# Low parts of the attention's weights by an adding transfer from DRAM

## The chip, the cores and the metric

One core of a Trainium2 chip runs the whole program. The metric is the device time of one execution in microseconds (us). Five engines work side by side, each through its own list of instructions in order: TensorE (PE, and PEld for its weight loads), VectorE (DVE), ScalarE (ACT), GpSimd (POOL) and SyncE (SP). SP, ACT and POOL also issue DMA transfers.

## What is computed

Two network blocks over 256 tokens of width 1024: a block with a latent attention (MLA) and a state-space layer (S5), then a block with a mixer, a cross attention and a feed-forward part. The change lies in the MLA layer, whose projections are

```python
q_dn, kv_dn, k_rope, gate = jnp.split(h @ w_in, MLA_SPLITS, axis=-1)
q = (_rmsnorm(q_dn, q_norm) @ w_uq).reshape(b, n, MLA_HEADS, MLA_NOPE + MLA_ROPE)
q_abs = jnp.einsum('bnhd,chd->bnhc', q[..., :MLA_NOPE], w_uk)
...
return (v * jax.nn.silu(gate)) @ w_out
```

## The kernel before

Matrix products of float32 are made of three passes on PE: every operand is split into a high part (`hi`, rounded to the float32r type) and a low part (`lo = x - hi`), and `mm` (L116 to L121) adds hi*hi, lo*hi and hi*lo, one matmul a line (L119, L120, L121).

A weight tile is 128x1024 (512 KB). `weight` (L88) takes it in: SP loads `wr` from DRAM (three buffers), ACT writes `wh` (L97), DVE subtracts `wl = wr - wh` (L98). `wh` and `wl` have two buffers each in the ring "w", so the tiles of a weight are free for the next but one only when its last matmul is done.

The MLA layer has two stages. In `mla_in` 16 gate tiles are made, each by 24 matmuls of 512 columns over one weight (`linear`, tile `lin`), then ACT takes the result (`sg`, L738) and SP stores it. In `mla_heads` 16 heads are worked on, with one weight of `hp` for two heads (`pair_in`, tile `qrope` first) and the first twelve weights of `w_out1` (`mla_out`). That makes 16 + 8 + 12 = 36 weights.

Beside it runs the preparation of the S5 layer, `s5_prep`, cut into pieces that `side` puts between the gates and heads. One pass (16 in all) loads `sp_x`, and for each of two directions d makes two outer products on DVE: `sp_r`, and `sp_o`, a single buffer of which ACT writes one slice (L390) and DVE the rest, and which SP stores to DRAM as `d_o`. Then PE transposes `sp_r` (tile `rtps`, L400), ACT copies that out (`sp_rt`, L404, two buffers, stored as `d_rt`), and PE multiplies `sp_o` with `sp_r` (tile `gps`, L413). After the second direction ACT copies `gps` to `sp_g` (L419), and POOL issues eight stores `d_t` of 64 KB (L427).

PE keeps the order of the program (`self.ordered`): gate, the modulation's matmuls `modps`, `rtps`, `gps`, the next gate, and so on, one direction a gate. The order on DVE, ACT, POOL and SP is the framework's list scheduler's, by priority; the outer products stand at a lower priority (`behind`).

Of the kernel before, what the change touches and what calls it, by code (L numbers as in the profile page):

```python
# [11 lines left out]
F32 = mybir.dt.float32  # L12
# [7 lines left out]
ADD, SUB, MUL, MAX, MIN = ALU.add, ALU.subtract, ALU.mult, ALU.max, ALU.min  # L20
# [8 lines left out]
class InOrder:  # L29


    def __init__(self, net, engine):
        self.net, self.engine = net, engine
# [6 lines left out]
class Net:  # L40
    def __init__(self, tc, ctx, I, out):
        self.tc, self.nc, self.ctx, self.I, self.out = tc, tc.nc, ctx, I, out
        self.dram = ctx.enter_context(tc.tile_pool(name="scratch", bufs=1, space=DRAM))
        self.gp = ctx.enter_context(tc.tile_pool(name="glob", bufs=1))
        self.big = ctx.enter_context(tc.tile_pool(name="big", bufs=1))
        self.ordered = ()
        nc = self.nc
        self.ident = self.gp.tile([128, 128], F32, name="ident")
        make_identity(nc, self.ident)
        self.ones = {}  # L50
        for n in (1, 1024, 512):
            t = self.gp.tile([128, 128], F32, name=f"ones{n}")
            nc.gpsimd.memset(t, 1.0 / n)
            self.ones[n] = t
# [33 lines left out]
    def weight(self, src, keep=None):  # L88


        nc = self.nc
        pool, tag, bufs = keep or self.rings[0]
        self.rings.append(self.rings.pop(0))
        raw = self.wp.tile([128, 1024], F32, tag="wr", name="wr", bufs=self.nwts[0])
        hi, lo = (pool.tile([128, 1024], F32R, tag=tag + x, name=tag + x, bufs=bufs) for x in "hl")
        nc.sync.dma_start(raw, src)
        self.in_order(nc.scalar.copy(hi, raw))  # L97
        self.in_order(nc.vector.tensor_tensor(lo, raw, hi.bitcast(F32), SUB))  # L98
        return hi, lo

    def split(self, hi, lo, x):
# [976 lines left out]
    def s5_layer(self, h1):  # L1078
# [3 lines left out]
        with self.tc.tile_pool(name="s5", bufs=1) as tp:  # L1082
# [52 lines left out]
            for b, (nu, early, late) in enumerate(((5, 0, 1), (3, 0, 1), (2, 1, 1), (0, 12 - NG, 0))):  # L1135
# [8 lines left out]
                for a in range(max(nu, 4 if prev else 0)):  # L1144
                    if a < nu:
                        u(*next(todo))
                        run(scan, 4.0)
                    for _ in range((early + 3 - a) // 4):
                        gate(1)
                        run(scan, 2.6)  # L1150
                    if prev and a < 4:
                        within(a)
                        across(a)
                        run(scan, 2.7)
# [422 lines left out]
    def run(self):  # L1577
        nc, tc, I = self.nc, self.tc, self.I
        self.s5_scratch()
        self.d_sg = self.dram.tile([16, 128, 512], F32, name="d_sg")  # L1580
        z = self.big.tile([128, 8, 512], F32, tag="s16", name="z", bufs=3)
        m0, m1 = (self.gp.tile([128, 24, 2], F32, name=f"mod{i}") for i in range(2))
        merged = ExitStack()
        merged.enter_context(self.phase((3, 2), ps=6, bg=2))
        with tc.tile_pool(name="prep", bufs=1) as prep:
            self.cond()

            def background():
                for k in range(16):
                    yield from self.s5_prep(k, prep)  # L1590

            def mods():
                yield from self.mod(0, [1], m0, prep)
                yield from self.mod(1, [0, 1], m1, prep)

            pieces, rest, due = background(), mods(), [D0, 0]

            def side(n):

                next(rest, None)  # L1600
                due[0] += n
                while due[0] >= 0.5 and due[1] < 64 - 2 * NL:
                    due[0] -= 0.5
                    due[1] += 1
                    if next(pieces):
                        break

            def step():
                with self.pinned("DVE"):
                    next(pieces, None)  # L1610

            with tc.tile_pool(name="lamp", bufs=1) as lp:
                lam = self.s5_lambda(self.s5_lambda_in(lp), prep, lp)

                def beside(n):
                    for _ in range((2, 1, 1, 2)[n]):
                        next(lam)

                self.ordered = (mybir.EngineType.PE, mybir.EngineType.DVE, mybir.EngineType.Activation)
                with tc.tile_pool(name="mod0", bufs=1) as mp:  # L1620
                    act, first = self.start(z, m0, mp, beside)
                self.ordered = (mybir.EngineType.PE,)
                with self.behind():
                    for _ in lam:
                        pass
                    self.s5_consts(prep)
            self.cos = self.load(self.gp, I["cos"], [128, 256], "cos")
            self.sin = self.load(self.gp, I["sin"], [128, 256], "sin")
            self.qnw = self.load(self.gp, I["q_norm"], [128, 2], "qnw")
            nc.vector.tensor_scalar(self.qnw, self.qnw, MLA_SCALE, None, MUL)  # L1630
            self.kvn = self.load(self.gp, I["kv_norm"], [128, 1], "kvn")
            side(1)
            with tc.tile_pool(name="mla", bufs=1) as mla:
                q = self.mla_in(z, act, first, mla, side)
                with tc.tile_pool(name="mlah", bufs=1) as tp:
                    vg = self.mla_heads(z, m0, q, tp, side)
            d_x1 = self.dram.tile([128, 8, 256], F32, name="d_x1")
            for _ in rest:
                pass
            with tc.tile_pool(name="ln", bufs=1) as tp:  # L1640
                h1 = self.ln_mod(z, vg, m0, m1, d_x1, tp, step)
            for _ in pieces:
                pass
        with tc.tile_pool(name="ops", bufs=1) as self.ops:
            y = self.s5_layer(h1)
        res = merged.enter_context(tc.tile_pool(name="res", bufs=1))
        x1 = res.tile([128, 8, 256], F32, name="x1")
        nc.sync.dma_start(x1, d_x1)
        with tc.tile_pool(name="mem", bufs=1) as mp:
            K, V, fill, norm = self.mem_kv(mp)  # L1650
            self.ordered = (mybir.EngineType.PE,)
            self.rings.append((mp, "w", 2))
            with tc.tile_pool(name="glu", bufs=1) as tp:
                self.glu(y, m1, x1, tp, fill, norm)
            g = self.load(mp, I["xa_g"], [128, 8], "xag")
            with tc.tile_pool(name="att", bufs=1) as ap:
                fg = self.load(mp, I["ffn_g"], [128, 8], "ffg")
                first = self.pre(x1, g, ap, X_SCALE)
                with tc.tile_pool(name="mix", bufs=1) as tp:
                    self.mixer(x1, tp, fill, first[1])  # L1660
                with tc.tile_pool(name="up", bufs=1) as fp:
                    second = self.pre(x1, fg, fp)
                    with tc.tile_pool(name="xat", bufs=1) as tp:
                        self.xattn(x1, K, V, tp, first[0], first[1], first[2], fill, second[1])
                    with tc.tile_pool(name="ffn", bufs=1) as tp:
                        g = tp.tile([128, 1024], F32, name="fing")
                        nc.sync.dma_start(g, I["fin_g"].partition_broadcast(128))
                        acc, h = self.ffn(x1, tp, second[0], second[1], second[2])
                        self.final(h, acc, g, tp)
        merged.close()  # L1670
# [119 lines left out]
```

## Time and profile before

| | us |
|---|---|
| median of 3 runs | 1449.93 (1447.34 to 1457.54) |
| the profiled execution | 1449.68 |
| its span, first to last instruction | 1447.9 |

| engine | busy, us | share of the span |
|---|---|---|
| PE | 1328.2 | 92% |
| DVE | 1150.6 | 79% |
| ACT | 712.2 | 49% |
| POOL | 102.9 | 7% |

The profile lists, for each group of instructions, its line in the code, engine and tiles (out<-in), the count, the busy time and the mean duration, and the engine's idle time before them with what ended it. Views of the trace give the same for a stretch of time; a stretch is named by its microseconds from the start of the span. The gates of `mla_in` run from 57 to 203 us, the heads from 207 to 511 us.

### The profile page before, as it was taken

The page shows a single profiled execution, that of the slowest core. Times are in us where ns is not written, and L with a number is a line of the kernel's source. Part 1 is how long each engine was busy: PE and PEld are TensorE (multiplying, and loading weights), DVE is VectorE, ACT ScalarE, POOL GpSimd, SP SyncE. Part 2 cuts the span into 40 slices and gives each one's busy share as a digit, 9 for nine tenths or more (in the row PEclk, how much of TensorE's full clock was granted, in tenths as well). Part 3 has the DMA queues.
Part 4 walks back from the last instruction along what each step waited for, and adds up shares of the span by engine and source line. Part 5 has one row for each costly group of instructions (what it writes and reads, how often), then busy time and mean ns, then how long its engine had stood idle before and what let it go on. Part 6 is the DMA issues. An engine that isn't in the chain of part 4 may idle for free.

```text
span 1447.9 us, 31095 instructions
## 1 busy us (share of the span) xinstructions
PE 1328.2 (92%) x12512; PEld 1196.9 (83%) x12512; DVE 1150.6 (79%) x2123; ACT 712.2 (49%) x1308; POOL 102.9 (7%) x225
## 2 busy tenths in 40 slices
PE   5879979999999988988768699999999999999997
PEld 4656657888888887888757599999998999999996
DVE  7999888998888899389898766555578876888887
ACT  4424436765656536322333264444347556655554
POOL 0012221111001100111111000000000000000000
PEclk9989988999999998999898899999999999999999
DMA  9469996665455544797778665655555453555552
GB/s 347 165 197 282 294 280 168 183 178 157 156 159 158 163 124 154 236 315 256 256 269 298 252 228 181 209 196 193 189 166 180 154 182 103 179 188 188 189 183 96
DMA packets 140625, 291.40 MB, mean 201 GB/s; under 512 B 30480, under 2 KB 70080, under 8 KB 135104
## 3 DMA queue, kind: packets, MB, share of 16 engines
q1 hardware_dynamic: 108592, 232.01, 48.2%
q0 software_dynamic: 11360, 49.34, 10.9%
q10 hardware_dynamic: 20528, 8.06, 2.1%
q8 instruction: 98, 1.61, 0.4%
q14 instruction: 47, 0.39, 0.1%
HBM read 234.83 MB, written 54.53 MB: 200 GB/s over the span
## 4 chain that ended last, share of the span: by engine, by line
PE 67%; DVE 20%; DMA 7%; issue 3%; ACT 3%; SPq 0%; DVEq 0%; ACTq 0%
PE lin L120 14%; PE lin L121 14%; PE lin L119 14%; DVE s_t L493 4%; DVE wl L98 3%; PE vps L472 2%; DVE s_V L495 2%; DMA sp_x<-in_s_bcw_dram 2%; DVE sp_t L37 2%; DMA mraw<-in_w_mod_dram 1%; PE dn L121 1%; PE dn L119 1%; PE dn L120 1%; DMA d_o<-sp_o 1%; DVE s_V L497 1%
## 5 line engine op out<-in xcount | busy, mean ns | idle before, releaser
L97 ACT CAST wh<-wr 128x1024 fp32r<-128x1024 f32 x268 | 280.7, 1049 | 405.4 <-PE lin L120 258.0
L98 DVE TENSOR_TENSOR wl<-wr,wh 128x1024 fp32r<-128x1024 f32 x268 | 327.6, 1223 | 146.3 <-ACT wh L97 145.6
L119 PE MATMUL lin<-prH,wh 128*128 128x256 f32 x512 | 145.3, 284 | 0.0
L119 PE MATMUL lin<-yaH,wh 128*128 128x256 f32 x512 | 144.9, 283 | 0.0
L120 PE MATMUL lin<-yaL,wh 128*128 128x256 f32 x512 | 144.7, 283 | 0.0
L121 PE MATMUL lin<-prH,wl 128*128 128x256 f32 x512 | 143.7, 281 | 1.0 <-DVE wl L98 1.0
L120 PE MATMUL lin<-prL,wh 128*128 128x256 f32 x512 | 144.1, 281 | 0.4 <-DVE prL L109 0.2
L121 PE MATMUL lin<-yaH,wl 128*128 128x256 f32 x512 | 144.2, 282 | 0.0
L120 PEld LDWEIGHTS lin<-prL,wh 128*128 128x128 f32 x512 | 96.6, 189 | 2.1 <-DVE prL L109 1.0
L119 PEld LDWEIGHTS lin<-yaH,wh 128*128 128x128 f32 x512 | 97.6, 191 | 0.0
L121 PEld LDWEIGHTS lin<-yaH,wl 128*128 128x128 f32 x512 | 97.5, 190 | 0.0
L119 PEld LDWEIGHTS lin<-prH,wh 128*128 128x128 f32 x512 | 96.7, 189 | 1.0
L120 PEld LDWEIGHTS lin<-yaL,wh 128*128 128x128 f32 x512 | 97.4, 190 | 0.0
L121 PEld LDWEIGHTS lin<-prH,wl 128*128 128x128 f32 x512 | 96.2, 188 | 1.2 <-DVE wl L98 1.2
L493 DVE TENSOR_TENSOR s_t<-s_V,s_tab 128x256 f32<-128x256 f32 (+2 forms) x120 | 73.1, 652 | 16.0 <-ACT s_V L475 14.7
L121 PE MATMUL u<-h,wl 128*128 128x256 f32 x224 | 64.1, 286 | 9.7 <-DVE wl L98 9.6
L121 PE MATMUL lin<-h,wl 128*128 128x256 f32 x128 | 43.2, 338 | 32.2 <-DVE wl L98 32.2
L427 POOL DMA_DIRECT2D d_t<-sp_g x128 | 67.0, 531 | 59.6 <-DVE sp_g L37 55.4
L119 PE MATMUL u<-h,wh 128*128 128x256 f32 x224 | 64.0, 286 | 0.0
L120 PE MATMUL u<-h,wh 128*128 128x256 f32 x224 | 63.3, 283 | 0.0
L119 PE MATMUL lin<-hH,wh 128*128 128x512 f32 x144 | 60.9, 423 | 0.7 <-ACT hH L103 0.7
L37 DVE TENSOR_TENSOR sp_t<-s_pb,sp_x 128x1024 f32<-128x1024 f32 x64 | 59.9, 953 | 0.6
(505 smaller groups left out, 3837.2 us busy)
## 6 DMA issues: line engine op xcount, KB each, us to landing
wr<-in_glu_dram SPq DMA_DIRECT2D x64, 512.0 KB, 3.3
wr<-in_w_up_dram SPq DMA_DIRECT2D x44, 512.0 KB, 3.3
wr<-in_w_in_dram SPq DMA_DIRECT2D x32, 512.0 KB, 4.8
mraw<-in_w_mod_dram SPq DMA_DIRECT2D x64, 256.0 KB, 3.3
d_rt<-sp_rt SPq DMA_DIRECT2D x64, 256.0 KB, 4.1
d_o<-sp_o SPq DMA_DIRECT2D x32, 512.0 KB, 4.7
wr<-in_s_in_dram SPq DMA_DIRECT2D x32, 512.0 KB, 4.4
s_op<-d_o POOLq DMA_DIRECT2D x16, 1024.0 KB, 7.3
```

The source lines that it names most:

```text
L37: return lambda *a, **k: self.net.in_order(f(*a, **k))
L97: self.in_order(nc.scalar.copy(hi, raw))
L98: self.in_order(nc.vector.tensor_tensor(lo, raw, hi.bitcast(F32), SUB))
L119: self.in_order(t.matmul(out, a[0], b[0], start=start, stop=False))
L120: self.in_order(t.matmul(out, a[0], b[1], start=False, stop=False))
L121: self.in_order(t.matmul(out, a[1], b[0], start=False, stop=stop))
L427: nc.gpsimd.dma_start(self.d_t[k].rearrange("s i j e c -> i s j e c")[:, :, j, e], a)
L472: self.in_order(nc.tensor.matmul(p[64 * e:64 * e + 64, c:c + 64], rt[:, d, j, r, 64 * e:64 * e + 64], u, start=True, stop=True, skip_group ...
L493: go(v.tensor_tensor(t[:, x], src.to_broadcast([128, 2, 32, n]), a[x].unsqueeze(1).to_broadcast([128, 2, 32, n]), MUL))
L495: go(v.tensor_tensor(dst, dst, t[:, 0], ADD))
L497: go(v.tensor_tensor(dst[:, 1], dst[:, 1], t[:, 1, 0], ADD))
```

## The change

While the MLA layer is issued (a flag that `run` sets around `mla_in` and `mla_heads`), DVE no longer makes `wl`. ACT writes `wl = -wh`, and POOL issues a transfer from the weight's place in DRAM that adds the weight onto `wl`. All other weights are made as before.

```diff
-        self.ordered = ()
+        self.ordered, self.adding = (), False
...
         self.in_order(nc.scalar.copy(hi, raw))
-        self.in_order(nc.vector.tensor_tensor(lo, raw, hi.bitcast(F32), SUB))
+        if self.adding:
+
+            nc.scalar.mul(lo, hi.bitcast(F32), -1.0)
+            nc.gpsimd.dma_start(lo, src, accum_op=ADD)
+        else:
+            self.in_order(nc.vector.tensor_tensor(lo, raw, hi.bitcast(F32), SUB))
         return hi, lo
...
+            self.adding = True
             with tc.tile_pool(name="mla", bufs=1) as mla:
                 q = self.mla_in(z, act, first, mla, side)
                 with tc.tile_pool(name="mlah", bufs=1) as tp:
                     vg = self.mla_heads(z, m0, q, tp, side)
+            self.adding = False
```

Lines of before from L99 on stand five further down (L390 is L395, L427 is L432). PE's order stays. The scheduler's order on the other engines moves.

On ACT, in the gates, one pass of `s5_prep` (two directions, so two gates) read before:

```order
L390 ACTIVATE sp_o<-sp_x 128x8x16
L97 CAST wh<-wr 128x1024
L738 ACTIVATE sg<-lin 128x512
L404 COPY sp_rt<-rtps 128x512 x2
L390 ACTIVATE sp_o<-sp_x 128x8x16
L97 CAST wh<-wr 128x1024
L738 ACTIVATE sg<-lin 128x512
L404 COPY sp_rt<-rtps 128x512 x2
L357 ACTIVATE sp_x<-sp_x 128x2x64
L419 COPY sp_g<-gps 128x240 x2
```

and reads now:

```order
L395 ACTIVATE sp_o<-sp_x 128x8x16
L97 CAST wh<-wr 128x1024
L743 ACTIVATE sg<-lin 128x512
L409 COPY sp_rt<-rtps 128x512 x2
L100 ACTIVATE wl<-wh 128x1024
L97 CAST wh<-wr 128x1024
L743 ACTIVATE sg<-lin 128x512
L409 COPY sp_rt<-rtps 128x512 x2
L100 ACTIVATE wl<-wh 128x1024
L395 ACTIVATE sp_o<-sp_x 128x8x16
L424 COPY sp_g<-gps 128x240 x2
L362 ACTIVATE sp_x<-sp_x 128x2x64
```

The negation (L100) stands behind the two copies of `rtps`, and the slice of `sp_o` for the second direction, which stood ahead of `wh`, now stands behind the second negation. `gps` of that direction reads the slice. The pattern is there for seven passes or parts of one.

On POOL, between two passes, stood before (`sp_r` is a small fill of the single buffer of that name):

```order
L385 MEMSET sp_r 128x16 x2
L427 DMA d_t<-sp_g 16x8x128 x8
L385 MEMSET sp_r 128x16 x2
L427 DMA d_t<-sp_g 16x8x128 x8
L385 MEMSET sp_r 128x16 x2
```

and stands now:

```order
L101 DMA wl<-in_w_in_dram 128x1024
L390 MEMSET sp_r 128x16
L101 DMA wl<-in_w_in_dram 128x1024
L390 MEMSET sp_r 128x16
L432 DMA d_t<-sp_g 16x8x128 x8
L101 DMA wl<-in_w_in_dram 128x1024
L390 MEMSET sp_r 128x16
L101 DMA wl<-in_w_in_dram 128x1024
```

Each adding transfer is issued behind a fill of `sp_r` or the eight stores of `d_t`.

## Rows read from the trace of the kernel before

**Rows 1.** DVE's subtractions, 55:500: xcount | busy us, mean ns | idle before
```profile
L98 DVE TENSOR_TENSOR wl<-wr,wh 128x1024 fp32r<-128x1024 f32 x36 | 43.8, 1220 | 1.1 <-ACT wh L97 1.1
```
**Rows 2.** Stretches: length; PE, PEld, DVE, ACT, POOL busy; clock, DMA share, GB/s
```profile
56.00:111.00 55.00, 45.93 (x340) 33.00 (x339) 50.56 (x90) 19.07 (x35) 6.66 (x16) 0.91 0.58 175
111.00:197.50 86.50, 80.47 (x736) 59.43 (x736) 76.39 (x106) 33.43 (x67) 22.07 (x50) 0.98 0.98 296
197.50:310.00 112.50, 103.89 (x914) 84.42 (x907) 99.93 (x184) 71.89 (x166) 17.52 (x39) 0.92 0.68 195
310.00:500.00 190.00, 190.00 (x1537) 157.26 (x1537) 163.26 (x299) 114.00 (x245) 17.65 (x40) 1.00 0.54 160
```
**Rows 3.** PE's waits, 56:111: total us, times, longest
```profile
PE rtps L400 <- DVE rs_t L156: 4.5, 1, 4.5
PE gps L413 <- DVE sp_o L37: 2.6, 2, 1.6
PE gps L413 <- DVE rs_t L156: 1.7, 1, 1.7
```
**Rows 4.** PE's waits, 111:197.5
```profile
PE gps L413 <- DVE sp_o L37: 3.5, 4, 1.6
```
**Rows 5.** PE in order of time, two gate ends: start us, us, instruction [idle before]
```profile
149.80 0.39 PE L121 MATMUL lin<-hH,wl 128*128 128x512 f32 x1
...
158.19 0.39 PE L121 MATMUL lin<-hH,wl 128*128 128x512 f32 x1
...
158.87 1.09 PE L400 MATMUL rtps<-ident,sp_r 128*128 128x128 f32 x8
159.89 0.81 PE L413 MATMUL gps<-sp_o,sp_r 64*32 64x128 f32 x32
160.62 0.50 PE L119 MATMUL lin<-hH,wh 128*128 128x512 f32 x1
```
**Rows 6.** ACT in order of time over the same gates
```profile
150.78 1.03 ACT L97 CAST wh<-wr 128x1024 fp32r<-128x1024 f32 x1
151.72 0.59 ACT L738 ACTIVATE sg<-lin 128x512 f32<-128x512 f32 x1
152.22 1.22 ACT L404 COPY sp_rt<-rtps 128x512 f32<-128x512 f32 x2
158.90 0.31 ACT L390 ACTIVATE sp_o<-sp_x 128x128 f32<-128x128 f32 x1 [5.46 <-DMA d_o<-sp_o]
```
**Rows 7.** DMA, 111:197.5: all packets; issues with KB each, us to landing
```profile
DMA packets 19567, 25.56 MB, mean 296 GB/s; under 512 B 1670, under 2 KB 11910, under 8 KB 19557
...
d_o<-sp_o SPq DMA_DIRECT2D x11, 512.0 KB, 6.4
...
wr<-in_w_in_dram SPq DMA_DIRECT2D x7, 512.0 KB, 5.5
```
**Rows 8.** DMA issues, 310:500
```profile
wr<-in_w_out_dram SPq DMA_DIRECT2D x11, 512.0 KB, 3.6
```
**Rows 9.** DMA issues of POOL, whole program
```profile
s_op<-d_o POOLq DMA_DIRECT2D x16, 1024.0 KB, 7.3
```
**Rows 10.** POOL's time to issue transfers, whole program
```profile
L427 POOL DMA_DIRECT2D d_t<-sp_g x128 | 67.0, 531 | 59.6 <-DVE sp_g L37 55.4 <-issue 2.6 <-DVE rs_t L157 1.7
```
**Rows 11.** In the heads: ACT's copy of a `hp` weight, and PE's first use of its low part
```profile
322.72 1.06 ACT L97 CAST wh<-wr 128x1024 fp32r<-128x1024 f32 x1 [1.90 <-PE lin L120]
...
333.30 0.39 PE L121 MATMUL qrope<-qnH,wl 128*128 128x512 f32 x1
```
**Rows 12.** The first gate's weight: ACT's copy, and PE's first use of the low part
```profile
52.33 1.05 ACT L97 CAST wh<-wr 128x1024 fp32r<-128x1024 f32 x1
...
57.54 0.40 PE L121 MATMUL lin<-hH,wl 128*128 128x512 f32 x1
```
**Rows 13.** DVE's waits, 111:197.5
```profile
DVE sp_x L37 <- DMA sp_x<-in_s_bcw_dram: 6.7, 5, 2.6
```

## Prediction

> **What bounds the kernel now.** I first split the MLA layer into stretches and looked, in each, at PE, which keeps the program's order, and at what it waits for [rows 2]. From 310 to 500 us, in the heads, PE is busy for 190.0 of 190.0 us at clock 1.00: nothing that another engine saves can be gained there. From 56 to 111 us PE is idle for 55.0 - 45.9 = 9.1 us, from 111 to 197.5 us (ten gates) for 86.5 - 80.5 = 6.0 us, from 197.5 to 310 us for 112.5 - 103.9 = 8.6 us. DVE is busy for about nine tenths of all these stretches, which suggests that it is the bound, so I read PE's waits. Ahead of 111 us they name DVE, 4.5 + 2.6 + 1.7 = 8.8 us [rows 3]. Between 111 and 197.5 us DVE is named for only 3.5 us [rows 4], and there another resource is full: the DMA engines are busy for 0.98 of the time at 296 GB/s [rows 2], and a store `d_o` of 512 KB, whose single buffer `sp_o` must be free before the next direction starts, takes 6.4 us to land [rows 7].
>
> **What goes: DVE's subtractions.** 36 of 1.22 us, 43.8 us of DVE [rows 1]. They can give back no more than PE waits for DVE: 8.8 us ahead of 111 us, 3.5 us up to 197.5 us, and an unknown part of the 8.6 us behind that. The upper bound is thus 8.8 + 3.5 + about 4 = 16 us, the lower one nothing. Ahead of 111 us part of the gain is lost at once. The first gate's weight is copied by 53.4 us (52.33 + 1.05), and PE wants its low part at 57.54 us [rows 12]; with a negation of 1.05 us, an issue of 0.53 us [rows 10] and some 5.5 us until it lands, it comes near 60.5 us, 3 us late, and the statistics that DVE waits for come behind that gate. I take -3 us for this stretch, all 3.5 us for the next, and -1 us for the last: **-7.5 us**. DVE also meets fewer waits for `sp_x`, 6.7 us in five passes now [rows 13], but PE shows these only through the 3.5 us that are counted.
>
> **What is added on ACT.** A negation has the shape of the copy of `wh`, 1.03 us [rows 6]; 36 make 37 us, and ACT is busy for 33.4 of 86.5 us in the gates [rows 2], so the busy time as such is covered. The place is not. In the order of after, the slice of `sp_o` for a pass's second direction stands behind gate result, two copies of `rtps` and the negation, and `gps` of that direction reads it. In the rows, the gate ahead of such a `gps` ends at 158.19 + 0.39 = 158.58 us, the slice was written at 158.90 us, ahead of all copies, and `gps` started at 159.89 us, when `rtps` was done (158.87 + 1.09) [rows 5]. In the gate before, ACT needed 2.66 us from the start of `wh` (150.78) to the end of both copies (152.22 + 1.22) [rows 6]. Put behind a gate end at 158.58 us, the copies end near 161.4 us, the negation near 162.4 us, the slice near 162.7 us, and `gps` starts 2.8 us later than it did. PE has nothing else to do, since its order is fixed, and the next gate stands behind it. It happens once a pass, seven times: **+19.6 us**. It is nothing only if PE would have waited for DVE or for `d_o` at that place anyway; then the wait at the other direction's `gps`, 3.5 us in all, is what it replaces, and that is already in the first term.
>
> **What is added to the DMA.** 36 transfers of 512 KB, 18.9 MB. From 310 us on the engines are busy for 0.54 of the time [rows 2], and PE covers them. Between 111 and 197.5 us ten come to 5.24 MB on top of 25.56 MB [rows 7]. If the DMA engines set the pace there, that is 5.24 / 0.296 = 17.7 us; if the 0.98 only counts packets that wait for each other, it is nothing. Five of the seven stalls lie in this stretch and lengthen it by 14 - 3.5 = 10.5 us anyhow, to 97 us, in which 28.7 MB pass at 296 GB/s; 30.8 MB need 104 us. I take a little over half of the 7 us that are left, since single slices of the trace run well above the mean: **+4 us**.
>
> The Trainium skill (DMA: Bandwidth & Descriptors, Rules for kernel authors) says that an accumulating DMA reads its destination and writes it later. No adding transfer is in this trace to compare. As an estimate by that page, each would move 512 KB more, the stretch 36.0 MB or 122 us in place of 104, and with the same share of the rest the sum would come to some 1477 us.
>
> **When the low part is there.** An adding transfer of 512 KB has no row. The nearest are plain loads of that size from SP, 3.6 us where the engines are half idle [rows 8] and 5.5 us in the gates [rows 7], and POOL's loads of twice the size, 7.3 us [rows 9]. I take 7 us in the gates and 6 in the heads, with 3.6 as the lower end and 12 us, more than twice the loaded SP load, as the upper. In the gates a weight's buffer is free at one gate's end (149.80 + 0.39 = 150.19 us) and its low part is wanted about 0.6 us after the start of the gate after the next (160.62 us) [rows 5], 11 us later, and 13.8 us with the new stall. Copies and negation take 2.66 + 0.6 + 1.0 = 4.3 us of it, the issue 0.5 us [rows 10], so 9.0 us are left for the landing: 7 us fit. What POOL has ahead of it (the fill of `sp_r`, which waits for a `gps` one gate earlier, and eight stores of 0.53 us each [rows 10]) ends before the buffer is free. In the heads, a copy that starts at 322.72 us when the buffer comes free feeds a use at 333.30 us [rows 11]; of these 10.6 us, copy, two other copies, negation and issue take about 4, so 6.6 us are left against 6. Four `hp` weights are that close; I add **+1 us**, and nothing for the rest.
>
> **The sum.** -7.5 + 19.6 + 4 + 1 = +17.1 us on the profiled execution's 1449.68 us: 1466.8 us, in round numbers 1467. The median of the runs, 1449.93 us, is the same within 0.3 us.
>
> **The rivals.**
>
> *Hidden.* The loop through `sp_o` (6.4 us to land plus DVE's two writes) already takes nearly a gate, so a PE that is held at one direction's `gps` may find less to wait for at the other, and the stall then costs about 1 us a pass net. For it speaks that ACT's slice was itself released by `d_o` [rows 6]; against it, that PE did not wait at that place [rows 5]. 1449.7 - 7.5 + 7 + 1 = 1450 us, up to 1455.
>
> *The transfer is late.* If an adding transfer needs more than the 9.0 us that the gates leave, PE stops at the first L126 (before's L121) of each gate; a buffer turns round once in two gates, so each us more costs half a us in each of 14 gates, 7 us in all, and in the heads (left: 6.6 us) a us at each of four weights. At 10 us: 7 + 3.4 x 4 - 1 = 20 us more, 1487 us. For it speaks the full DMA and that the transfer must combine two operands; against it, that POOL's loads of twice the size land in 7.3 us [rows 9].
>
> *DVE is the bound after all.* PE's waits on DVE go entirely, the stall on ACT does not show, because DVE's own product ends still later than the slice, and the new transfers hide: 1449.7 - 16 = 1434 us. It decides if `gps` in the gates waits for nothing that ACT wrote. For it speaks DVE's share of nine tenths [rows 2]; against it, that PE waits for DVE for only 3.5 us over ten gates [rows 4].
>
> **How the numbers follow.** The forecast, 1455 to 1480 us, gets 0.45, hidden 0.30, late 0.15, DVE as the bound 0.10. A change of over 1% is about what a measurement of this kernel can tell from none: above 1464.4 or below 1435.4 us. Of the forecast's 0.45 about 0.33 lies above 1464.4 us, with the late transfer 0.48: slower. Faster is the last rival, 0.10; the rest, 0.42, is within 1%. The range reaches down over the hidden case, with some gain left (-16 plus half the stall, 1444 us), and up to the full DMA term and a moderately late transfer: 1449.7 - 3 + 19.6 + 17.7 + 6 = 1490 us. It leaves out DVE as the bound and half of the late transfers.
>
> **What would show it.** In the profile after: DVE lighter by 44 us and PE's busy time in the heads unchanged; in the gates a wait of PE at `gps` of nearly 3 us, once a pass, released by ACT's `sp_o` (if it names DVE or nothing, the second term is wrong); landing times of the adding transfers below 9 us (above it, PE waits at L126 for DMA); the stretch from 111 us to the last gate longer by 10 to 18 us at no more than 300 GB/s. The forecast fails if the stall is covered, or if the adding transfer is several times as slow as a load.

## The result, and the profile after

The changed kernel takes 1494.34 us (median; 1491.15 to 1494.69), the kernel before 1449.04 us beside it: ratio 1.030, 95% interval 1.027 to 1.032. It is slower, as forecast, but by 45 us and not by 17; 1494 lies just above the range that ended at 1490 us.

Nearly all of the loss is made ahead of the first scores of the heads. TensorE keeps the program's order, so the first scores of the first head (`slat`) mark the end of the same work in every kernel that keeps the paces of the background work. The views of this group in the kernel before, and then in the changed one, give count, min/median/max ns, and the first and last start:

```profile
L119 PE MATMUL slat<-ckH,qaH x32: 392/474/797, 220.2 to 483.5; 128*128 128x512 f32 x32
```

```profile
L124 PE MATMUL slat<-ckH,qaH x32: 392/474/797, 263.7 to 527.4; 128*128 128x512 f32 x32
```

The first scores come 43.5 us later, the last ones 43.9 us later: the heads themselves, bound by PE, take as long as before. The stretches of the changed kernel, which answer to [rows 2]:

```profile
56.00:111.00 55.00, 44.52 (x304) 32.66 (x304) 42.99 (x81) 22.25 (x37) 11.20 (x22) 0.91 0.80 205
111.00:197.50 86.50, 65.49 (x503) 47.92 (x503) 45.90 (x68) 29.27 (x53) 23.34 (x45) 0.84 0.94 255
...
310.00:500.00 190.00, 188.65 (x1569) 156.15 (x1562) 153.71 (x300) 129.75 (x274) 28.73 (x52) 1.00 0.74 195
```

From 111 to 197.5 us VectorE fell from 76.4 to 45.9 us of 86.5, so the relief is there, and TensorE fell with it, from 80.5 to 65.5 us. The DMA engines are the only ones that stay full: a share of 0.94, but 255 GB/s where [rows 2] has 296. They are nearly as busy as before and move less. What TensorE waits for between 56 and 260 us (sum, times, longest; [rows 3, 4] answer):

```profile
PE gps L418 <- DVE sp_o L37: 31.4, 10, 5.3
PE qabs L124 <- ACT waH L108: 4.4, 1, 4.4
PE lin L126 <- DMA wl<-in_w_in_dram: 4.3, 1, 4.3
PE gps L418 <- ACT sp_o L395: 4.3, 2, 2.1
```

It names VectorE, but VectorE itself waits, in the same stretch:

```profile
DVE sp_o L37 <- DMA d_o<-sp_o: 55.4, 14, 7.3
DVE sp_x L37 <- DMA sp_x<-in_s_bcw_dram: 12.7, 6, 4.5
```

The store `d_o`, whose single buffer must be free before the next direction's product, took 6.4 us to land [rows 7]; in the changed kernel, from 111 to 250 us (KB each, median us to landing):

```profile
d_o<-sp_o SPq DMA_DIRECT2D x11, 512.0 KB, 9.4
wl<-in_w_in_dram POOLq DMA_DIRECT2D x10, 512.0 KB, 9.0
wr<-in_w_in_dram SPq DMA_DIRECT2D x7, 512.0 KB, 4.6
```

How much of the DMA engines an adding transfer takes can be read from the list of queues (packets, MB, share of all 16 engines over the span). `q0` is POOL's, before and after:

```profile
q0 software_dynamic: 11360, 49.34, 10.9%
```

```profile
q0 software_dynamic: 16544, 68.21, 17.1%
```

17.1% of 1492.3 us less 10.9% of 1447.9 us is 97 us of all 16 engines for 36 transfers: **2.7 us for one**, if the other transfers of that queue cost what they did. That number, times the number of transfers in the gates, is what the experiments turn on.

The theories: **A**, the adding transfer's engine time lengthens the work of DMA engines that are full in the gates; **B**, the new order on ScalarE and SyncE costs the time, whatever is moved; **C** is A put more sharply, each us of engine time costs about a us in the gates even if nobody waits for the transfer; **D**, only what stands on a path costs (the wait for the low part, POOL's queue); **E**, the landing of `d_o` costs, through the single buffer of `sp_o`.

### The profile page after: what moved, and what is told of

It is laid out like the page before. It is cut to its first block, busy times and chain, and to the rows that moved or that the text cites. A ratio compares the mean times of both kernels' runs of the same rounds, so it can differ in the third digit from the quotient of the medians.

```text
span 1492.3 us, 31158 instructions
## 1 busy us (share of the span) xinstructions
PE 1347.6 (90%) x12512; PEld 1212.6 (81%) x12512; DVE 1111.6 (74%) x2087; ACT 742.7 (50%) x1344; POOL 135.9 (9%) x261
## 3 DMA queue, kind: packets, MB, share of 16 engines
q0 software_dynamic: 16544, 68.21, 17.1%
HBM read 253.70 MB, written 54.53 MB: 207 GB/s over the span
## 4 chain that ended last, share of the span: by engine, by line
PE 62%; DVE 14%; DMA 11%; issue 10%; ACT 2%; POOL 1%; SPq 0%; DVEq 0%; ACTq 0%; POOLq 0%
PE lin L126 13%; PE lin L124 13%; PE lin L125 13%; DMA d_o<-sp_o 6%; DVE s_t L498 3%; DVE wl L103 2%; PE dn L126 1%; DVE s_V L500 1%; PE dn L124 1%; PE dn L125 1%; DMA s_op<-d_o 1%; PE vps L477 1%; DVE sp_t L37 1%; PE modps L596 1%; DVE sp_o L37 1%
## 5 line engine op out<-in xcount | busy, mean ns | idle before, releaser
L103 DVE TENSOR_TENSOR wl<-wr,wh 128x1024 fp32r<-128x1024 f32 x232 | 283.7, 1224 | 146.0 <-ACT wh L97 145.6
L432 POOL DMA_DIRECT2D d_t<-sp_g x128 | 68.8, 578 | 55.7 <-DVE sp_g L37 33.9
L124 PE MATMUL lin<-hH,wh 128*128 128x512 f32 x144 | 67.4, 468 | 0.7 <-ACT hH L108 0.7
L126 PE MATMUL lin<-hH,wl 128*128 128x512 f32 x144 | 63.0, 437 | 4.3 <-DMA wl<-in_w_in_dram 4.3
L124 PE MATMUL u<-h,wh 128*128 128x256 f32 x224 | 66.1, 295 | 0.0
L125 PE MATMUL u<-h,wh 128*128 128x256 f32 x224 | 65.5, 292 | 0.0
```

The lines of the kernel that those rows point to most:

```text
L124: self.in_order(t.matmul(out, a[0], b[0], start=start, stop=False))
L125: self.in_order(t.matmul(out, a[0], b[1], start=False, stop=False))
L126: self.in_order(t.matmul(out, a[1], b[0], start=False, stop=stop))
L432: nc.gpsimd.dma_start(self.d_t[k].rearrange("s i j e c -> i s j e c")[:, :, j, e], a)
```

## The experiments

### In which stage

`e1_gates` sets the flag for `mla_in` alone (its diff stands here), `e2_heads` for `mla_heads` alone:

```diff
             self.adding = True
...
                 q = self.mla_in(z, act, first, mla, side)
+                self.adding = False
```

> The adding transfers in the gates alone, the heads' and output weights with VectorE's subtraction as before. All theories that put the loss into the gates: the changed kernel's time, 1485 to 1497. A loss that is spread over gates and heads by the number of weights (8 or so of 36 are the gates') would give 1455 to 1465.

Measured: 1486.9 us (ratio 1.027, 1.022 to 1.031). Its first scores start at 262.9 us.

> The adding transfers in the heads alone, the gates as before. If the loss is the gates' alone: 1444 to 1454, no difference to the kernel before, since the heads are bound by TensorE. If adding transfers cost wherever they run (contention, landing): 1465 to 1485.

Measured: 1455.9 us (1.002, 1.000 to 1.005), 2 us above the range for a loss of the gates alone. The loss is mainly the gates', 35 us of it by themselves. Yet the first scores of `e2_heads` started at 229.5 us, 9 us late, ahead of any score; that was taken up again below.

### Order or traffic

The three kernels here keep the order of the changed one on the engines (but for a few neighbours). They leave out all or part of the low part, so they serve for timing alone. `e3_plain` overwrites where the change adds; `e4_piece` adds an eighth of the columns; `e7_half`, run later, adds one half.

```diff
-            nc.gpsimd.dma_start(lo, src, accum_op=ADD)
+            nc.gpsimd.dma_start(lo, src.bitcast(F32R))                              (e3_plain)
+            nc.gpsimd.dma_start(lo[:, 0:128], src[:, 0:128], accum_op=ADD)          (e4_piece)
+            nc.gpsimd.dma_start(lo[:, 0:512], src[:, 0:512], accum_op=ADD)          (e7_half)
```

> The changed kernel, whose POOL transfer overwrites the low part with the weight instead of adding (so the low parts are not subtracted); same order on all engines, same bytes out of DRAM, same dependences, only the kind of transfer differs. Theory A (the adding transfer takes about 327 ns for 4 KB where a plain one takes 159, and that lengthens the landing of the store of sp_o, which sets the gates' pace): about half of the 45 us goes, 1460 to 1475, landing of d_o back to about 7 us. Theory B (the loss is the new order on ScalarE and SyncE's queue, whatever is transferred): 1485 to 1497. If bytes alone are what crowds, B's time too, but with d_o's landing still at 9 to 10 us.

Measured: 1475.3 us (1.017, 1.014 to 1.020), and 8.0 us for the landing of `d_o` (56 to 260 us; 9.4 in the changed kernel). With the same order 19 us are gone, so theory B can't explain the whole loss.

> The changed kernel, whose adding transfer moves the first 128 of 1024 columns alone (the other columns' low part is left without the weight); order on the engines as in the changed kernel, an eighth of the traffic. Theory A (traffic of the adding transfers): 1450 to 1465, what is left being the order: d_o issued about 1.9 us behind VectorE's sp_o in each direction, 6.4 us landing, 9.6 us a direction against 8.4 to 9.2. Theory B (order alone): 1485 to 1497. Between the two, the share of each can be read off.

Measured: 1453.8 us (1.0025, 1.0005 to 1.0044). With an eighth of the columns, nearly nothing is lost: the order, with the negations and with VectorE's relief set against them, costs some 2 us. Theory B is out. TensorE's waits in this kernel, 57 to 250 us:

```profile
PE gps L418 <- ACT sp_o L395: 8.9, 4, 2.5
PE gps L418 <- DVE sp_o L37: 8.8, 6, 3.4
...
PE lin L126 <- ACT qf L756: 1.6, 1, 1.6
```

The stall that I forecast at `gps`, released by ACT's slice of `sp_o`, is there, up to 2.5 us each time, but four times and not seven. The wait of 4.5 us for VectorE's statistics [rows 3] is gone.

> The changed kernel, whose adding transfers move 512 of the 1024 columns (the other half of the low parts is left without the weight); order as in the changed kernel. Theory C, price in proportion to what is moved: e4_piece's 1454 at 1/8 and 1494 at 8/8 give 1466 to 1476 at 4/8. A theory of slack used up (the store of sp_o lands inside its slack until a threshold): below 1460, or above 1485.

Measured: 1469.4 us (1.012, 1.008 to 1.016): about in proportion to what is moved; the three sizes show no threshold.

### Traffic that nobody waits for

`e5_extra` and `e6_extra_add` take the kernel before, VectorE's subtraction and all, and add for each gate a POOL transfer onto a tile that is never read; in `e11_extra_act` ScalarE issues it.

```diff
         self.in_order(nc.vector.tensor_tensor(lo, raw, hi.bitcast(F32), SUB))
+        if self.wx:                                  (the making of the two tiles wx is not shown)
+            self.wx.append(self.wx.pop(0))
+            nc.scalar.copy(self.wx[0][:, 0:1], hi.bitcast(F32)[:, 0:1])
+            nc.gpsimd.dma_start(self.wx[0], src)         (e6_extra_add: accum_op=ADD; e11: nc.scalar)
```

> The kernel before, with its subtraction on VectorE, and for each of the 16 gates one more plain POOL transfer of the gate's weight (512 KB) into a tile that nobody reads (a copy of one column on ScalarE ties its start to the high part). Theory C (the 16 DMA engines are full in the gates, and each byte added there costs its engine time, whoever waits for it): 128 packets of 4 KB over 16 engines at 159 ns are 1.27 us, times 16 is 20 us: 1466 to 1480. Theory D (only what stands on the path costs: the wait for the low part, the new order, the queue of POOL): 1448 to 1456.

> The same as the one before it, the 16 transfers onto the unread tiles being adding ones. Theory C with the packets' time from the changed kernel: 8 packets of 327 ns are 2.6 us, times 16 is 42 us: 1485 to 1500, as slow as the changed kernel though nothing waits for them. Theory C with bytes instead of engine time as what counts: as e5_extra, 1466 to 1480. Theory D: 1448 to 1456.

Measured: 1466.3 us (1.010, 1.006 to 1.014) and 1480.0 us (1.020, 1.015 to 1.024). Both speak for C, and the 13.7 us between them, at the same bytes, against a price by bytes. But the second lies below the range of C, 1485 to 1500, at the upper end of that for bytes. And the trace of `e5_extra` shows a wait that the experiment brought itself:

```profile
PE gps L417 <- POOL sp_r L389: 15.0, 5, 3.9
```

POOL's fill of `sp_r` stood behind a transfer that waited for its copy on ScalarE, so these two kernels by themselves don't tell C from D. Hence the third, without POOL:

> As e5_extra, but the 16 plain transfers onto unread tiles are issued by ScalarE, so that nothing on POOL's queue stands behind them (in e5_extra TensorE waited 15.0 us for POOL's memset of sp_r, which was queued behind such a transfer). Theory C: 13 of the 16 fall into the stretch whose engines are 0.98 busy, times 1.27 us, 16 us: 1462 to 1472. Theory E: landing of d_o grows a little, 1450 to 1460. If e5_extra's 15 us were POOL's queue alone: 1448 to 1455.

Measured: 1468.9 us (1.013, 1.010 to 1.016). There neither POOL nor ScalarE releases what TensorE waits for at `gps` (56 to 240 us; VectorE's wait in the kernel before came to 7.6 us from 56 to 220):

```profile
PE gps L417 <- DVE sp_o L37: 15.9, 9, 4.0
```

Plain transfers onto unread tiles still cost 19 us. Theory D is out, for plain transfers. For adding ones without POOL's queue it was not tried: by the Trainium skill (DMA: Bandwidth & Descriptors, SWDGE vs HWDGE vs iDMA) GpSimd alone issues them; no run here shows it.

### The sum over all of them

The stretch from 56 us to the first scores, in the view by stretches, of before, `e7_half`, `e3_plain` and the changed kernel (columns as in [rows 2]):

```profile
56.00:220.20 164.20, 142.02 (x1164) 103.83 (x1163) 144.64 (x223) 61.52 (x118) 33.13 (x76) 0.92 0.84 251
```

```profile
56.00:242.10 186.10, 148.93 (x1162) 109.47 (x1161) 124.94 (x206) 76.70 (x136) 49.67 (x94) 0.89 0.89 243
```

```profile
56.00:245.90 189.90, 149.29 (x1169) 109.40 (x1167) 125.97 (x207) 77.52 (x137) 43.83 (x95) 0.91 0.88 264
```

```profile
56.00:263.70 207.70, 156.22 (x1165) 114.08 (x1164) 125.87 (x205) 77.10 (x136) 49.86 (x95) 0.86 0.91 242
```

Length times DMA share is the engines' busy time: 138 us before, 189 us in the changed kernel. The table sets this against the price of one added transfer, worked out from the queues' shares as above, and against the delay:

| kernel | one added transfer, us of all engines | DMA busy, 56 us to first scores | more than before | first scores later by |
|---|---|---|---|---|
| before | | 138 | | |
| e4_piece | 0.48 | 142 | 4 | 2.3 |
| e5_extra | 1.5 | 156 | 18 | 15.2 |
| e11_extra_act | 1.6 | 160 | 22 | 19.4 |
| e7_half | 1.45 | 166 | 28 | 21.9 |
| e3_plain | 1.5 | 167 | 29 | 25.7 |
| e6_extra_add | 2.8 | 181 | 43 | 32.8 |
| changed kernel | 2.7 | 189 | 51 | 43.5 |

Some 0.75 to 0.9 of every us that the engines are kept busy longer appears as delay, over kernels that differ in the order, in who waits, and in which queue issues (`e4_piece` apart, whose 4 us are too few to read). Where the share is near 0.9 throughout, a longer stretch gives more busy time by itself, so the sums matter that come from elsewhere: the changed kernel's 51 us are 18 transfers of 2.7 us (16 of `w_in`, and two of the first `hp` weights), the 22 us of `e11_extra_act` are 16 of 1.6 us, less some 3. Nor does the price come from the crowd: an adding packet of 2 KB in `e7_half` took 178 ns in the median both from 111 to 250 us (DMA share 0.95) and from 330 to 480 us (0.65), SP's plain packets of 2 KB 84 ns in both.

Three kernels don't fit. In `e16_after_g3`, below, the engines are busy 37 us more and the first scores 46.7 us later, in `e2_heads` 4 and 9.3 us, in `e13_heads_late` 1 and 5.2 us: there a part of the delay has other causes than the load.

`e7_half` and `e3_plain` are the sharpest pair: half the columns added take the engines as long as all of them copied, and cost about as much. What counts is thus engine time and not bytes.

Of the 43.5 us only 29 are idle time of TensorE. The other 14 are its own busy time for the same instructions (142.0 and 156.2 us): the mean granted clock fell from 0.92 to 0.86, which is a mean over its two levels, 2.4 and 1.2 GHz. Behind the first gate's wait, from 62 to 70 us, it is near the lower one (0.58):

```profile
62.00:70.00 8.00, 7.53 (x20) 6.01 (x21) 3.21 (x5) 1.24 (x2) 2.03 (x5) 0.58 0.40 89
```

Whether this slower work added to the delay, or only filled time in which the DMA engines set the pace, no run here separates.

### Is it the one buffer of `sp_o`?

The chain of waits of the changed kernel gives `d_o` 57.6% of the stretch from 100 to 250 us. So a second buffer was tried, in the changed kernel and in the one before; `wr` gives up one of three buffers, and `uvr` moves into `wr`, for the room (that line is not shown).

```diff
-        merged.enter_context(self.phase((3, 2), ps=6, bg=2))
+        merged.enter_context(self.phase((2, 2), ps=6, bg=2))
...
-                O = tp.tile([128, 2, 4, 9, 16], F32, name="sp_o")
+                O = tp.tile([128, 2, 4, 9, 16], F32, name="sp_o", bufs=2)
```

> The changed kernel with two buffers of sp_o instead of one (and two of wr instead of three, and uvr put into one of them, for the room), so that VectorE's and ScalarE's next sp_o need not wait for the landing of the store before. Theory E (the price of the added transfers is the longer landing of that store, 6.1 us before and 9.4 after, in a loop through one buffer): most of the 45 us goes, 1450 to 1465. Theory C (the engines' load itself is the bound, and the loop only shows it): their share of 0.94 can grow to 1 at most, so some 10 us go, 1478 to 1490.

> The kernel before with the same two buffers of sp_o, two of wr and uvr in wr's, as the control. Either theory: VectorE waits 3.8 us for that store in the gates now, so at most that is gained, and with two buffers of wr the weights come later by up to a landing of 5.5 us here and there: 1445 to 1460.

Measured: 1538.9 us (1.061) and 1497.7 us (1.033), both outside every range. Both pay some 46 us behind the first scores, most likely for the buffer of `wr`, which serves all layers; that was missed in the expectation. Against each other they can be read: 1538.9 - 1497.7 = 41 us, where one buffer has 45. At the first scores it is 257.4 - 223.6 = 34 us in place of 43.5. VectorE's wait for `d_o` is gone from the head of the list of `e9_after_o2`, and others stand in its place (56 to 258 us, TensorE, then VectorE):

```profile
PE rtps L405 <- DVE sp_r L37: 23.2, 3, 9.3
PE lin L126 <- DMA wl<-in_w_in_dram: 20.5, 8, 4.5
```

```profile
DVE sp_x L37 <- DMA sp_x<-in_s_bcw_dram: 33.9, 4, 9.9
```

So with these buffers the second one for `sp_o` regains no more than a quarter: this speaks for C and against E. It doesn't bound E with three buffers of `wr`: the waits that are last now, TensorE's for adding transfers among them (eight times, 20.5 us), may come in part of the tighter room.

### Relief for the gates

`e8_after_s75` moves background work out of the gates.

```diff
-G1, G2, NL, D0, NG = 1,0.28,2,-1.0,5
+G1, G2, NL, D0, NG = 0.75,0.335,2,-1.0,5
```

> The changed kernel with a quarter of the gates' background work (4 of 16 directions) moved into the heads, by the paces G1 0.75 and G2 0.335 instead of 1 and 0.28. Theory C: a direction's transfers (d_o, two d_rt, half of sp_x, four d_t) take some 5 us of all engines, so the gates lose 20 us, and the heads gain 4 times 1.8 us of transposes and gps: 1475 to 1487. If the loss hangs on something else than the load of the DMA engines in the gates: 1490 to 1500, or more, since heads are bound by TensorE.

Measured: 1480.9 us (1.021, 1.015 to 1.026), the expected amount: with the adding transfers left as they were, 13 us come back when other work leaves the gates. That work is TensorE's and VectorE's too, so the kernel before is needed beside it: with the same pace in the gates (`e15_before_s75b`, below) its first scores come 16.0 us earlier, those of the changed kernel 24.5 us. The 8.5 us between them are what fits C.

`e12_heads_s75` has the same paces on top of `e2_heads`.

> A try at a kernel faster than before: adding transfers in the heads alone (DMA engines 0.54 busy there, VectorE freed of 20 subtractions) and a quarter of the gates' background work moved into the heads (G1 0.75, G2 0.335). The gates' DMA engines lose 20 us of work, of which TensorE's 80.5 of 86.5 us leave 5 to 10 to be gained; the heads gain 4 times 1.8 us of TensorE's work: 1442 to 1455. If the moved work fits worse: up to 1465.

Measured: 1454.4 us (1.004, 1.002 to 1.006), no gain. The first scores came at 206.6 us, 13.6 us earlier than before, and the last at 476.3, 7.2 us earlier, and by the end all was lost again, most likely because the background work ended too late; no run changes that alone.

### What was still open

`e13_heads_late` sets the flag in `mla_heads`, behind the first pair:

```diff
         queries(0)
+        self.adding = True
         out = None
...
-            self.adding = True
             with tc.tile_pool(name="mla", bufs=1) as mla:
```

> As e2_heads (adding transfers in the heads alone), but they begin behind the first pair's weights, whose loads are ahead of time in the gates. In e2_heads the first head's scores began at 229.5 us against 220.2 before, though its gates subtract as before. Theory C: that was 3 adding transfers of 2.6 us in the last, full stretch of the gates; now 1446 to 1453, with the first scores at 219 to 223. If adding transfers in the heads cost by themselves: 1453 to 1459 as e2_heads.

Measured: 1457.3 us (1.006, 1.005 to 1.008): C's range is missed, and the time lies in the other one, by which adding transfers in the heads cost by themselves. The first scores came at 225.4 us, 4 us better than in `e2_heads` but 5 us late. The trace shows that another transfer, of the next pair, took the place: POOL issued an adding one at 210.22 us, as the last gate's result was being stored, and ScalarE's first cast of the heads waited for that store.

```profile
210.22 0.95 POOL L101 DMA_DIRECT2D wl<-in_hp_dram  x1 [0.96 <-ACT wl L100]
```

```profile
220.00 0.58 ACT L108 CAST qfrH<-qrope 128x512 fp32r<-128x512 f32 x1 [4.13 <-DMA d_sg<-sg]
```

In the kernel before, this cast started at 213.83 us and waited 0.32 us for the same store. That is a cost at the seam between gates and heads, but no run isolates it, and the DMA engines are no fuller there than before (share 0.84 from 203 to 221 us, before 0.86). Another 3.6 us go between the first and the last scores (266.9 us against 263.3), 2.2 of them in one wait of TensorE for an adding transfer of a `hp` weight; the changed kernel itself loses only 0.4 us there.

> The changed kernel, with the first three gates' low parts subtracted by VectorE as before. The first gate waited 4.3 us for its adding transfer to land, and the engines were 0.58 busy before in 56 to 111, so theory C has no price for load there: the wait alone goes, 1486 to 1492. If each adding transfer costs its engine time wherever it stands in the gates, 3 times 2.6 us more go: 1479 to 1486.

```diff
             def gate(h):
+                self.adding = h > 2
```

Measured: 1496.6 us (1.034, 1.032 to 1.035): missed both ways, no gain at all. The first gate's wait is gone, but the order has shifted, and TensorE waits elsewhere (56 to 260 us):

```profile
PE rtps L405 <- DVE sp_r L37: 28.9, 4, 13.8
PE lin L126 <- DMA wl<-in_w_in_dram: 10.8, 6, 3.2
```

One of these is 13.8 us long, behind the last gate, where the DMA share is 0.63 only (241 to 267 us). There VectorE, which works in order, stood ahead of `sp_r` at another instruction, `uvL`, whose chain goes back to the load of `uvr`:

```profile
251.29 0.40 ACT L108 CAST uvH<-uvr 128x256 fp32r<-128x256 f32 x1 [8.87 <-DMA uvr<-in_uv_dram]
251.73 0.42 DVE L109 TENSOR_TENSOR uvL<-uvr,uvH 128x256 fp32r<-128x256 f32 x1 [14.01 <-ACT uvH L108]
```

So this run says nothing about load in the first gates; it says that the 4.3 us at the first gate can't be counted on.

The last two change the paces, on top of `e13_heads_late` and in the kernel before:

```diff
-G1, G2, NL, D0, NG = 1,0.28,2,-1.0,5
+G1, G2, NL, D0, NG = 0.75,0.365,2,-1.0,5
```

> A try at a kernel faster than before: as e13_heads_late, with paces G1 0.75 and G2 0.365, so that a quarter of the background work leaves the gates and is done by about the 50th of the heads' 54 calls, as before (e12_heads_s75 gained 13.6 us up to the first scores and lost them by the end, its background work ending with the last call). 1436 to 1446; if the heads' VectorE or TensorE pay for the moved work in full, 1447 to 1455.

> The kernel before with the same paces, as the control of e14_late_s75b: with VectorE still subtracting all low parts. VectorE has 220 us of 250 busy in 250 to 500 and would get 3 more directions of some 7 us: if that is too much, 1450 to 1465; if not, as e14_late_s75b, and the adding transfer has no part in the gain.

Measured: 1442.1 us (0.9956, 0.9939 to 0.9972) and 1443.9 us (0.9976, 0.9962 to 0.9990). Both beat the kernel before, by 6 and by 3.5 us, and the first of them also the changed kernel, by 52. The paces alone, with all subtractions left on VectorE, give more than half of it; the intervals overlap, so it isn't shown that the adding transfers in the heads have a part in the gain.

## Why the prediction was wrong

**What bounds the gates** was read rightly: the prediction names the DMA engines, 0.98 busy [rows 2], as the full resource between 111 and 197.5 us. The sum then did not go by it.

**The DMA term, +4 us, is the step that failed.** It was worth some 41 us (43.5 us in the changed kernel, less the 2.3 us of `e4_piece`). Four things in it were wrong. It priced bytes at the mean 296 GB/s, in place of the time for which a transfer keeps the engines busy: 2.7 us for an adding one, 1.5 for a plain one from the same queue, and with plain ones alone (`e3_plain`) the loss is 24 us. It counted ten transfers, those between 111 and 197.5 us, and not all 18 ahead of the first scores (at its own 296 GB/s, 18 would have made 32 us); what the first few cost by themselves, where the engines had been 0.58 busy, no run shows. It set 10.5 us of a forecast stall against the added traffic, as if the engines caught up in it, though that stall was itself uncertain. And it allowed that the 0.98 "only counts packets that wait for each other", from which came the lower bound of nothing; `e11_extra_act` shows that the engines had little room: 22 us of added work made 19.4 us of delay. The upper bound of 17.7 us came from the same bytes, so the range could not hold the result. The estimate by the Trainium skill (DMA: Bandwidth & Descriptors, Rules for kernel authors), that an accumulating DMA also reads its destination, led to 1477 us: the runs agree that an adding transfer costs more than a plain one, 2.7 us to 1.5, nearly the double. How that comes about inside the transfer, no run shows.

**The ACT term, +19.6 us, was too large.** Its mechanism is in the trace of `e4_piece` as described, a stall of up to 2.5 us at `gps` (2.8 forecast) released by ACT's `sp_o`, but four times, 8.9 us in all; in the changed kernel twice, 4.3 us, where mostly VectorE's product ends last. Together with VectorE's relief it came to 2 us, which is the net of the rival *hidden*, 1450 to 1455 us: without the traffic that rival would have been the result. That the total of the prediction had the right sign was the work of a term that was mostly not there.

**The gain from VectorE, -7.5 us,** can't be separated by these runs, but its largest part is seen: the 4.5 us for the statistics [rows 3] are gone in `e4_piece`, where two waits for statistics at another place, 2.6 us, are new. That the first gate would lose was right, but it lost more than 3 us: its low part was used at 62.47 us in place of 57.54 [rows 12], with a wait of 4.31 us for the transfer.

**The landing, +1 us,** held: 7 us were taken for the gates, 8.7 us is the median ahead of the first scores, with 9.0 us to spare, and TensorE waited for a low part once in the gates, at the first, and once between the first and the last scores, for 1.1 us. The rival *late transfer* did not come to pass. What landed late was another transfer, `d_o`; the prediction named its loop and then priced the added traffic without it. The issue takes POOL 0.88 us, not 0.53 [rows 10], which nothing waited for.

**What would show it:** VectorE's busy time fell by 39 us over the program, where 44 were named (the subtractions are gone, but its other work took 5 us longer), and the heads stayed the same, as said. The wait at `gps` names VectorE and not ACT, which by the prediction's own words makes the second term wrong. The bandwidth stayed under 300 GB/s, but the stretch up to the last gate grew by 46.7 us (its last matmul starts at 249.6 us, before at 202.9), not by 10 to 18. The last sentence of the prediction named the case: "if the adding transfer is several times as slow as a load"; twice was enough.

## What to carry to other kernels

Where the profile shows the DMA engines full in a stretch, price an added transfer by the time for which it keeps them busy, times all transfers that fall into the stretch, and put most of that on the path (here 0.75 to 0.9 of it), whether or not anything waits for that transfer. Don't net it against a stall that is only forecast, and don't take the tile that the chain of waits names for the cause: with a second buffer for it, the next transfer was late. Saving VectorE's time by a transfer needs engines with room; and in the heads, where they had room, TensorE was the bound and nothing was gained (`e2_heads`, 1.002).

## What the runs showed of the hardware that was not expected

- An adding transfer of 512 KB from DRAM onto SBUF kept all 16 DMA engines busy for 2.7 us, a plain one from POOL for 1.5 us and one issued by ScalarE for 1.6 us. Reads from HBM rose only by the 18.87 MB of the source (253.70 against 234.83 MB).
- The price falls a little less than the size: 1.45 us for half of the columns, but 0.48 us for an eighth of them, 18% of the price for 12.5% of the bytes.
- An adding transfer takes POOL 0.88 us to issue, a plain one of the same shape 0.55 us.
- With the share of the DMA engines at 0.94 in place of 0.98, they moved 255 in place of 296 GB/s: the share tells how full they are, the bandwidth depends on what they carry.
